# GpSimd's order of row gathers and indirect adds, written by an estimate of its time

## The chip, the cores and the metric

One core of one Trainium2 chip runs the kernel. The metric is device microseconds of one execution, the median of several runs. The engines are TensorE (PE, with its weight loads as PEld), VectorE (DVE), ScalarE (ACT), GpSimd (POOL) and the sequencer SyncE (SP), which issues most loads. Sixteen DMA engines move the data of all queues.

## The reference, cut to what matters

The layer has a token mixer (attention and a recurrent branch) and then PEER, a channel mixer that retrieves single-neuron experts. All of the change lies in PEER. For 256 tokens:

```python
q = (xt @ w_q).reshape(T, 8, 2, 128)                 # 8 heads, two halves
s = einsum('thcd,hcnd->thcn', q, sub_keys)           # 128 keys for each half
sv, si = top_k(s, 16)
cand = sv[:, :, 0, :, None] + sv[:, :, 1, None, :]   # 16 x 16 candidates
cv, ci = top_k(cand.reshape(T, 8, 256), 16)
idx = i1 * 128 + i2                                  # 16 of 16384 experts for each head and token
g = softmax(cv)
u = u_tab[idx]
act = gelu(einsum('td,ted->te', xt, u)) * g
out = einsum('te,ted->td', act, v_tab[idx])          # then residual add and a last RMSNorm
```

## The kernel before, in words

The token mixer fills the first 638 us. PEER follows in two phases.

**The u phase** is a list of 144 **units**, run in order u = 0 to 143. A unit streams one 1 MB tile of weights through TensorE. A query unit (`wq`, 16 of them, two for a head) makes a head's queries for all 256 tokens. A `u` unit (128 of them) multiplies 128 experts' rows of `u_tab` with the first TD = 192 tokens and stores the gelu of it. So for 192 tokens every expert is computed densely; the weights g are scattered into a dense matrix `G` in HBM (three tensors `g_d`, one for each 64 tokens), and later multiply the dense gelu.

**The v phase** (128 chunks of 1 MB, u = 144 to 271) multiplies the weighted gelu with `v_tab` densely.

The last 64 tokens go another way: their experts' rows are **gathered**. Each head has 8 gathers of 128 rows (1 MB each) from `u_tab`, 64 in all, and later as many from `v_tab`. VectorE takes a dot product of each gathered tile with the tokens (`dot`, L605), and in the v phase a scaled add (`axpy`, L623).

Work in one unit, in the order in which it is written (this order is the order on every engine; the section is scheduled by hand, `tc.manual_schedule()`):

1. TensorE: the unit's matmuls (L125). Then ACT copies a part of PSUM (`rest`, L798) and VectorE adds (`total`, L803). The `rest` copy marks a unit's end in the trace.
2. ACT rounds the tile of unit u+3 (`whi`, L566).
3. `want_rows(u)` (L594): GpSimd issues row gathers, while there are requests and one of the 4 `rows` buffers is counted as free (its dot was written two units earlier, or more).
4. `add_some`: GpSimd issues indirect adds to `g_d` (L635). A head has 24: 8 for each of the three tensors. The first add of a head to a tensor waits until all adds of the head before to that tensor have landed (`wait_for`).
5. `bg.run(budget)`: VectorE's retrieval steps (`retrieve`, the top-16 work of a head), while their written costs stay within a budget.
6. `use_rows(u, budget)`: the dots, each against a credit of 2.4, and only for rows requested at least LAG units earlier.
7. VectorE subtracts to get the low part of the tile of unit u+3 (`wlo`, L570). TensorE's unit u+3 needs it. SP then issues the load of unit u+7.

When a head's retrieval has finished, `spread` (called through `later`) sends its indices and weights to the tile `two`, from which both gathers and adds read, and appends 8 gathers to `wanted` and 24 adds to `to_add`.

`scores` (L679), the matmuls of a head's queries with its keys, stand behind a unit's matmuls, two units after the head's second query unit (`due`). At u = 135 and 137 SP loads the first tiles of `G` (`load_G`); the first of these loads waits for all adds of the last head. `weigh` and `weighed` at u = 140 and 141 prepare the first operand `a` of the v phase.

Of the kernel before, what the change touches and what calls it, by code (L numbers as in the profile page):

```python
# [22 lines left out]
HEADS = 8  # L23
# [8 lines left out]
KEEP = 6  # L32
BUDGET = 2.9
BUDGET_Q = 2.7
BUDGET_U = 1.05
ROWS_WQ = 0.5
ROWS_U = 1.0
ROWS_U2 = 1.35
ROWS_V = 1.25
ROWS = 4  # L40
RAW = 4
LAG = 4
PRIO = 300

# [34 lines left out]
def body(tc, A, out):  # L79
# [3 lines left out]
    with ExitStack() as es:  # L83
# [33 lines left out]
        def w_stationary(p, w, x, ks=range(KT), n=T):  # L117
            hi, lo = (t.rearrange("p (k c) -> p k c", c=128) for t in w)
            for k in ks:
                ins = [(p[:, 0:2 * n].rearrange("p (a t) -> p a t", t=n), hi[:, k], x[:, k, :, 0:n]),  # L120
                       (p[:, 0:n], lo[:, k], x[:, k, 0, 0:n])]
                if k == ks[-1]:
                    ins.reverse()
                for i, (d, a, m) in enumerate(ins):
                    pe.matmul(d, a, m, start=k == ks[0] and i == 0, stop=k == ks[-1] and i == 1)  # L125
# [10 lines left out]
        def bank(tag):  # L136
            return ps.tile([128, 512], F32, name=tag)
# [408 lines left out]

        units = [("wq", i) for i in range(6)]
        for h in range(3, HEADS):
            units += [("u", 10 * (h - 3) + i) for i in range(10)] + [("wq", 2 * h), ("wq", 2 * h + 1)]
        units += [("u", i) for i in range(10 * (HEADS - 3), 128)]  # L550
        stream = [A[name][i] for name, i in units]
        order = list(range(32 - KEEP, 32)) + list(range(32 - KEEP))
        stream += [A["v"][g, q] for g in order for q in range(4)]
# [2 lines left out]
        def fetch(i):  # L556
            if i < len(stream):
                raws[i] = (wp.tile([128, 2048], F32, name="raw") if i % RAW < 3 else
                           gp.tile([128, 2048], F32, name="raw4"))
                nc.sync.dma_start(out=raws[i], in_=stream[i].rearrange("p a b -> p (a b)"))  # L560

        def cut_hi(i, c=slice(0, 2048)):
            if i < len(stream):
                if i not in his:
                    his[i], los[i] = (wp.tile([128, 2048], F32R, name=n) for n in ("whi", "wlo"))
                act.activation(his[i][:, c], raws[i][:, c], AF.Copy)  # L566
# [5 lines left out]

        wanted, coming, later = [], [], []
        free, used = [0] * ROWS, []
        credit = 0.0

        def use_rows(u, budget):
            nonlocal credit
            for f in later:
                f()  # L580
            later.clear()
            credit = min(credit + budget, 3.0)
            while credit > 0 and coming and coming[0][0] <= u - LAG:
                _, t, f = coming.pop(0)
                f(t)
                used.append(u)
                credit -= 2.4

        def want_rows(u):
            while wanted and (free or used and used[0] <= u - 2):  # L590
                free.pop() if free else used.pop(0)
                table, idx, f = wanted.pop(0)
                t = gp.tile([128, D], F32, name="rows", bufs=ROWS)
                nc.gpsimd.indirect_dma_start(out=t, out_offset=None, in_=table,  # L594
                                             in_offset=bass.IndirectOffsetOnAxis(ap=idx, axis=0))
                coming.append((u, t, f))
# [34 lines left out]
        to_add = []  # L631
        added = {}

        def add_one(h, tt, at, gw):
            ins = nc.gpsimd.indirect_dma_start(  # L635
                out=cells[tt], out_offset=bass.IndirectOffsetOnAxis(ap=at, axis=0),
                in_=gw, in_offset=None, compute_op=ALU.add).ins
            mine = added.setdefault((h, tt), [])
            tc.add_to_no_dep_group(f"adds{h}{tt}", ins)
            if mine:  # L640
                tc.declare_no_dep(ins, group=f"adds{h}{tt}", reason="different experts of one head")
            elif h:
                wait_for(ins, h - 1, tt)
            mine.append(ins)

        def wait_for(ins, h, tt):
            for i in added[h, tt]:
                tc.add_manual_dep(ins, i.name, mybir.DependencyInfo(
                    mybir.DependencyClass.Sync, mybir.DependencyReason.DATA), reason="adds to G")

        def add_some(n):
            for _ in range(n):
                if to_add:
                    add_one(*to_add.pop(0))


        def spread(h, made):
# [17 lines left out]
        def scores(h, qT, keys):  # L675
            sp = bank("sx")
            for i in range(4):
                tt, c = i // 2, i % 2
                pe.matmul(sp[:, i * 128:(i + 1) * 128], qT[c][:, tt * 128:(tt + 1) * 128],  # L679
                          keys[:, c], start=True, stop=True)  # L680
            s = rp.tile([128, 4, 128], F32, name="s", bufs=2)
            act.activation(s.rearrange("p a n -> p (a n)"), sp, AF.Copy)
            bg.queue.append(retrieve(h, s))
# [53 lines left out]

        for i in range(3 + RAW):
            fetch(i)
# [12 lines left out]
        qT, due = [], []  # L752
        prods, Gs = {}, {}

        def load_G(m):
            Gs[m] = G = [vp.tile([128, 4, 64], F32, name=f"G{b}") for b in range(TD // 64)]
            g = order[m]
            for b in range(TD // 64):
                ins = nc.sync.dma_start(out=G[b], in_=g_d[b][:, 4 * g:4 * g + 4, :]).ins
                if m == 0:  # L760
                    wait_for(ins, HEADS - 1, b)

        def weigh(n):
            x, G = stash.pop(order[n]), Gs.pop(n)
            prods[n] = x
            for b in range(TD // 64):
                c = slice(64 * b, 64 * b + 64)
                dve.tensor_tensor(x[:, :, c], x[:, :, c], G[b], op=ALU.mult)
# [14 lines left out]
                stash[n] = x  # L783

        vp = None
        for u, (name, i) in enumerate(units):
            query = name == "wq"
            n = T if query else TD
            g, j = i // 4, i % 4
            if query and i % 2 == 0:  # L790
                keys = rp.tile([128, 2, 128], F32, name="keys")
                nc.scalar.dma_start(out=keys, in_=A["keys"][:, i:i + 2])
            p = bank("mm")
            w_stationary(p, (his.pop(u), los.pop(u)), hT, n=n)
            while due and due[0][0] <= u - 2:
                due.pop(0)[1]()
            rest = sm.tile([128, T], F32, name="rest")[:, 0:n]
            act.activation(rest, p[:, n:2 * n], AF.Copy)  # L798
            if query:
                y = rp.tile([128, T], F32, name=f"qT{i % 2}", bufs=1)  # L800
            else:
                y = sm.tile([128, T], F32, name="total")[:, 0:n]
            dve.tensor_tensor(y, p[:, 0:n], rest, op=ALU.add)  # L803
            cut_hi(u + 3)
            if query:
                qT.append(y)
                if i % 2:
                    due.append((u, lambda h=i // 2, q=qT, k=keys: scores(h, q, k)))
                    qT = []
            else:  # L810
                if j == 0:
                    st = stp.tile([128, 4, TD], F32, name="stash")
                act.activation(st[:, j], y, AF.Gelu_apprx_tanh)
                if j == 3:
                    if g < 32 - KEEP:
                        nc.scalar.dma_start(out=spill_d[g], in_=st)
                    else:
                        stash[g] = st
            busy = len(sel) < HEADS
            want_rows(u)  # L820
            add_some(2 if u % 4 else 1)
            bg.run(BUDGET_Q if query else BUDGET_U)
            use_rows(u, ROWS_WQ if query else ROWS_U if busy else ROWS_U2)
            if not busy and not to_add and vp is None:
                rp_cm.__exit__(None, None, None)
                kp_cm.__exit__(None, None, None)
                vp = es.enter_context(tc.tile_pool(name="v", bufs=2))
            if u == 135:
                load_G(0)
            if u == 137:  # L830
                load_G(1)
            if u == 140:
                weigh(0)
            if u == 141:
                a = weighed(0)
                refill(0)
            cut_lo(u + 3)
            fetch(u + 3 + RAW)
        assert not to_add and not bg.queue
# [20 lines left out]
        for n in range(31):  # L860
            for q in range(4):
                u = 144 + 4 * n + q
# [13 lines left out]
                cut_lo(u + 3)  # L876
                fetch(u + 3 + RAW)
            a = a1
# [146 lines left out]
```

## Time and profile before

| | us |
|---|---|
| median of 3 runs | 1984.75 |
| lowest and highest run | 1983.99, 1991.14 |
| the profiled execution | 1982.2 |
| span in its trace, first to last instruction | 1980.4 |

| engine | busy us | share of the span |
|---|---|---|
| PE | 1908.7 | 96% |
| DVE | 1550.9 | 78% |
| ACT | 972.4 | 49% |
| POOL | 705.9 | 36% |

Busy time is the union of an engine's instructions. A busy PE need not be at full speed, since its clock has two levels, and matmuls' ends are modelled. The shares are means over the whole kernel; which engine is late in a stage has to be read from that stage.

### The profile page before, as it was taken

What the parts mean: (1) busy time and instruction counts of PE and PEld (TensorE: products, weight loads), DVE (VectorE), ACT (ScalarE), POOL (GpSimd) and SP (SyncE); (2) the same over time, 40 slices, a digit from 0 to 9 for tenths busy, and PEclk for the clock granted to TensorE, in tenths of its full rate; (3) what the DMA queues carried; (4) which work ended last, traced back from release to release, by engine and by line L of the source; (5) the groups of instructions that cost most, each with busy time, mean ns of one, the idle gap of its engine ahead of it and who ended that gap; (6) DMA issues with size and microseconds to landing.
All of it is one profiled execution on the core that took longest, in us unless ns stands there. A gap on an engine that the chain in (4) does not pass through costs nothing. (4 is left out here: it accounts for less than half of the span.)

```text
span 1980.4 us, 26958 instructions
## 1 busy us (share of the span) xinstructions
PE 1908.7 (96%) x10570; PEld 1698.4 (86%) x10570; DVE 1550.9 (78%) x1884; ACT 972.4 (49%) x1115; POOL 705.9 (36%) x347
## 2 busy tenths in 40 slices
PE   7999999999999999999999889999999999999996
PEld 6888888888887899999999888899888888888884
DVE  7876655566556799999998666788888888888885
ACT  5554554444434555555565344455444444444443
POOL 1000000000000077888887888832332333233320
PEclk9999999999999999999999899999999999999998
DMA  7579555555555689999999989999999999999992
GB/s 294 194 264 331 189 207 191 180 185 190 193 211 184 227 306 344 302 302 302 331 317 318 290 306 318 342 406 389 369 410 402 379 392 407 408 384 390 379 395 86
DMA packets 142638, 594.71 MB, mean 300 GB/s; under 512 B 48768, under 2 KB 62128, under 8 KB 76464
## 3 DMA queue, kind: packets, MB, share of 16 engines
q1 hardware_dynamic: 82624, 422.72, 58.2%
q0 software_dynamic: 47936, 145.36, 20.8%
q10 hardware_dynamic: 11952, 24.92, 3.3%
q8 instruction: 83, 1.36, 0.3%
q14 instruction: 43, 0.35, 0.0%
HBM read 564.51 MB, written 28.68 MB: 300 GB/s over the span
## 5 line engine op out<-in xcount | busy, mean ns | idle before, releaser
L125 PE MATMUL mm<-hT,whi 128*128 128x384 f32 (+1 forms) x3328 | 1051.7, 378 | 0.2 <-ACT whi L93 0.2
L125 PE MATMUL mm<-hT,wlo 128*128 128x192 f32 (+1 forms) x3328 | 851.8, 266 | 35.9 <-DVE wlo L570 35.4
L125 PEld LDWEIGHTS mm<-hT,wlo 128*128 128x128 f32 x3328 | 638.9, 192 | 49.0 <-DVE wlo L570 41.0
L566 ACT ACTIVATE whi<-raw 128x2048 fp32r<-128x2048 f32 (+1 forms) x281 | 521.5, 1859 | 315.5 <-PE pv L857 205.4
L125 PEld LDWEIGHTS mm<-hT,whi 128*128 128x128 f32 x3328 | 622.0, 191 | 52.5 <-ACT hT L214 0.6
L570 DVE TENSOR_TENSOR wlo<-raw,whi 128x2048 fp32r<-128x2048 f32 (+1 forms) x281 | 620.9, 2217 | 37.9 <-ACT whi L566 37.9
L635 POOL DMA_INDIRECT g_d<-two x192 | 407.6, 2123 | 74.3 <-issue 70.0
L94 DVE TENSOR_TENSOR wlo<-raw,whi 128x2048 fp32r<-128x2048 f32 (+1 forms) x122 | 239.5, 1973 | 113.3 <-ACT whi L93 113.1
L594 POOL DMA_INDIRECT rows<-v_rows,two x64 | 173.8, 2716 | 382.9 <-DVE accv L623 349.2
L93 ACT ACTIVATE whi<-raw 128x2048 fp32r<-128x2048 f32 (+1 forms) x122 | 200.6, 1657 | 56.5 <-PE mm L114 49.8
L853 PE MATMUL pv<-whi,a 128*128 128x512 f32 x512 | 199.7, 390 | 1.0 <-DVE total L803 1.0
L857 PE MATMUL pv<-whi,a 128*128 128x512 f32 x512 | 200.3, 391 | 0.0
L858 PE MATMUL pv<-wlo,a 128*128 128x512 f32 x512 | 199.2, 389 | 0.0
L855 PE MATMUL pv<-wlo,a 128*128 128x512 f32 x512 | 199.2, 389 | 0.0
L854 PE MATMUL pv<-whi,a 128*128 128x512 f32 x512 | 199.2, 389 | 0.0
L605 DVE CUSTOM_DVE_ANT_0 rows<-rows,xg 128x2048 f32<-128x2048 f32 x64 | 146.2, 2285 | 58.8 <-DMA rows<-u_rows,two 58.8
L594 POOL DMA_INDIRECT rows<-u_rows,two x64 | 112.4, 1756 | 134.7 <-ACT rest L798 70.1
L623 DVE SCALAR_TENSOR_TENSOR accv<-rows,hid,accv 128x2048 f32<-128x2048 f32 x63 | 147.9, 2347 | 0.0
L132 ACT ACTIVATE rest<-mm 128x256 f32<-128x256 f32 x96 | 37.0, 385 | 212.4 <-PE mm L125 212.2
L798 ACT ACTIVATE rest<-mm 128x192 f32<-128x192 f32 (+1 forms) x144 | 48.1, 334 | 182.6 <-PE mm L125 180.7
L853 PEld LDWEIGHTS pv<-whi,a 128*128 128x128 f32 x512 | 96.1, 188 | 21.4 <-DVE total L803 1.3
L857 PEld LDWEIGHTS pv<-whi,a 128*128 128x128 f32 x512 | 96.3, 188 | 20.7 <-issue 0.8
(212 smaller groups left out, 1692.5 us busy)
## 6 DMA issues: line engine op xcount, KB each, us to landing
raw<-u SPq DMA_DIRECT2D x128, 1024.0 KB, 6.9
raw<-v SPq DMA_DIRECT2D x128, 1024.0 KB, 8.6
raw<-w_in SPq DMA_DIRECT2D x64, 1024.0 KB, 5.6
raw<-w_branch SPq DMA_DIRECT2D x16, 1024.0 KB, 5.6
raw<-w_out SPq DMA_DIRECT2D x16, 1024.0 KB, 4.9
raw<-wq SPq DMA_DIRECT2D x16, 1024.0 KB, 7.8
g_d<-zeros ACTq DMA_DIRECT2D x12, 1024.0 KB
G<-g_d SPq DMA_DIRECT2D x96, 128.0 KB, 9.9
```

Of the source, the lines that this page charges most:

```text
L93: return (act.activation(dst_hi, src, AF.Copy), dve.tensor_tensor(dst_lo, src, dst_hi.bitcast(F32), op=ALU.subtract))
L94: dve.tensor_tensor(dst_lo, src, dst_hi.bitcast(F32), op=ALU.subtract))
L125: pe.matmul(d, a, m, start=k == ks[0] and i == 0, stop=k == ks[-1] and i == 1)
L566: act.activation(his[i][:, c], raws[i][:, c], AF.Copy)
L570: dve.tensor_tensor(los[i][:, c], raws[i][:, c], his[i][:, c].bitcast(F32), op=ALU.subtract)
L594: nc.gpsimd.indirect_dma_start(out=t, out_offset=None, in_=table, in_offset=bass.IndirectOffsetOnAxis(ap=idx, axis=0))
L635: ins = nc.gpsimd.indirect_dma_start(out=cells[tt], out_offset=bass.IndirectOffsetOnAxis(ap=at, axis=0), in_=gw, in_offset=None, compute_o ...
L853: pe.matmul(p, a[:, j, 0:128], hi[:, j], start=first, stop=False)
L854: pe.matmul(p, a[:, j, 256:384], hi[:, j], start=False, stop=False)
L855: pe.matmul(p, a[:, j, 0:128], lo[:, j], start=False, stop=last)
L857: pe.matmul(p, a[:, j, 128:256], hi[:, j], start=first, stop=False)
L858: pe.matmul(p, a[:, j, 128:256], lo[:, j], start=False, stop=last)
```

## The change

The new code is in the section on PEER alone. It does these things:

- GpSimd's adds are no longer two in a unit (one in every fourth). A number `pool_at` estimates how far GpSimd has been given work, 2.1 us for a gather and 2.4 us for an add; `now` estimates when a unit ends, 5.6 us for a query unit and 4.6 us for a `u` unit. A unit first issues its gathers and then adds as long as `pool_at` lies before the unit's estimated end. From u = 137 on all remaining adds would be issued.
- There are 12 `u` units between two heads' query units, in place of 10.
- The budgets of retrieval and dots in a unit change a little.
- Rows are used at least five units after their request (LAG + 1) up to u = 143, in place of four.
- The scores of the first head stand one unit earlier.
- `load_G`, `weigh` and `weighed` stand one to three units later.

```diff
-BUDGET_U = 1.05
+BUDGET_U = 0.9
-ROWS_U = 1.0
-ROWS_U2 = 1.35
+ROWS_U = 1.08
+ROWS_U2 = 1.25
+UNIT_Q = 5.6
+UNIT_U = 4.6
+ADD_US = 2.4
+ROW_US = 2.1
...
-            units += [("u", 10 * (h - 3) + i) for i in range(10)] + [("wq", 2 * h), ("wq", 2 * h + 1)]
-        units += [("u", i) for i in range(10 * (HEADS - 3), 128)]
+            units += [("u", 12 * (h - 3) + i) for i in range(12)] + [("wq", 2 * h), ("wq", 2 * h + 1)]
+        units += [("u", i) for i in range(12 * (HEADS - 3), 128)]
...
-            while credit > 0 and coming and coming[0][0] <= u - LAG:
+            while credit > 0 and coming and coming[0][0] <= u - (LAG + 1 if u < 144 else LAG):
...
                 table, idx, f = wanted.pop(0)
+                pool_at += ROW_US
...
-        def add_some(n):
-            for _ in range(n):
-                if to_add:
-                    add_one(*to_add.pop(0))
+        def add_some(end):
+            nonlocal pool_at
+            while to_add and pool_at < end:
+                pool_at += ADD_US
+                add_one(*to_add.pop(0))
...
-            while due and due[0][0] <= u - 2:
+            while due and due[0][0] <= u - (2 if u > 2 else 1):
...
+            pool_at = max(pool_at, now)
+            now += UNIT_Q if query else UNIT_U
             want_rows(u)
-            add_some(2 if u % 4 else 1)
+            add_some(now if u < 137 else 1e9)
...
-            if u == 135:
+            if u == 138:
                 load_G(0)
-            if u == 137:
+            if u == 139:
                 load_G(1)
-            if u == 140:
+            if u == 141:
                 weigh(0)
-            if u == 141:
+            if u == 142:
```

GpSimd, from the first add of the last head on (the number behind `two` names a head's tile; the three `g_d` are the tensors of 64 tokens each). Before, from unit 106, with gathers of head 5 (counted from 0) between the adds:

```order
L635 DMA g_d_213<-two_10196 1048576x1
L635 DMA g_d_214<-two_10196 1048576x1
L635 DMA g_d_215<-two_10196 1048576x1
L635 DMA g_d_213<-two_10196 1048576x1
L594 DMA rows<-u_rows,two_8944 128x2048
L635 DMA g_d_214<-two_10196 1048576x1
L635 DMA g_d_215<-two_10196 1048576x1
L635 DMA g_d_213<-two_10196 1048576x1
L594 DMA rows<-u_rows,two_8944 128x2048
```

Now, from unit 116, the same adds, with gathers of head 6 between them:

```order
L642 DMA g_d_213<-two_10480 1048576x1
L642 DMA g_d_214<-two_10480 1048576x1
L601 DMA rows<-u_rows,two_9691 128x2048
L642 DMA g_d_215<-two_10480 1048576x1
L642 DMA g_d_213<-two_10480 1048576x1
L642 DMA g_d_214<-two_10480 1048576x1
L601 DMA rows<-u_rows,two_9691 128x2048
L642 DMA g_d_215<-two_10480 1048576x1
L642 DMA g_d_213<-two_10480 1048576x1
```

Three adds stand between two gathers in place of three or four, and at a given add of the last head the gathers are a head further on.

VectorE, the start of the u phase. Before, the query sums (`qT`) of units 0 to 3, and then the first retrieval steps:

```order
L803 TENSOR_TENSOR qT_5475<-mm,rest 128x256
L570 TENSOR_TENSOR wlo<-raw_5374,whi 128x2048
L803 TENSOR_TENSOR qT_5518<-mm,rest 128x256
L570 TENSOR_TENSOR wlo<-raw,whi 128x2048
L803 TENSOR_TENSOR qT_5563<-mm,rest 128x256
L570 TENSOR_TENSOR wlo<-raw,whi 128x2048
L803 TENSOR_TENSOR qT_5613<-mm,rest 128x256
L668 MAX sv<-s 128x8
```

Now:

```order
L813 TENSOR_TENSOR qT_5475<-mm,rest 128x256
L574 TENSOR_TENSOR wlo<-raw_5374,whi 128x2048
L813 TENSOR_TENSOR qT_5518<-mm,rest 128x256
L574 TENSOR_TENSOR wlo<-raw,whi 128x2048
L813 TENSOR_TENSOR qT_5570<-mm,rest 128x256
L677 MAX sv<-s 128x8
```

The retrieval of the first head starts in unit 2 in place of unit 3.

Written out unit by unit by the rules above, the two programs stand like this (numbers issued up to and with that unit):

| up to unit | dots before, now | gathers before, now | adds before, now |
|---|---|---|---|
| 87 | 30, 33 | 33, 36 | 137, 127 |
| 92 | 33, 35 | 36, 38 | 145, 134 |
| 121 | 49, 50 | 52, 53 | 192, 177 |
| 131 | 55, 55 | 58, 58 | 192, 192 |
| 143 | 62, 61 | 65, 64 | 192, 192 |

The first four gathers stand in unit 8 (before: 10), the last add in unit 131 (before: 119), and the last head's retrieval ends in unit 92 (before: 86). From unit 92 on a dot stands in about every second unit; of these 27 dots 8 stand five units behind their gather, 15 six and 4 seven. Before, of the 20 dots in units 90 to 124, 16 stand five units behind, 3 six and 1 seven.

## Rows read from the trace of the kernel before

**Rows 1.** All `rest` copies (L798): durations ns min/median/max, first and last start in us.
```profile
L798 ACT ACTIVATE rest<-mm x144: 308/332/387, 638.6 to 1370.6; 128x192 f32<-128x192 f32 x128, 128x256 f32<-128x256 f32 x16
```

**Rows 2.** Three stretches: us, busy (x instructions) by engine, PEclk, DMA share, GB/s.
```profile
691.90:1074.80 382.90, 376.24 (x2538) 365.69 (x2537) 369.67 (x649) 216.41 (x288) 311.77 (x154) 1.00 0.95 316
1074.80:1272.60 197.80, 171.36 (x1123) 169.13 (x1122) 132.20 (x114) 85.31 (x109) 170.08 (x87) 0.94 0.92 310
1272.60:1370.60 98.00, 97.86 (x671) 97.60 (x669) 83.39 (x73) 51.25 (x67) 39.29 (x18) 0.97 1.00 390
```

**Rows 3.** The first stretch, `rest` copies alone: ACT busy us and count.
```profile
691.90:1074.80 382.90, 26.06 (x78) 1.00 0.95 316
```

**Rows 4.** Waits in 1074.8 to 1272.6: us in total, times, longest.
```profile
PE mm L125 <- DVE wlo L570: 26.4, 7, 5.7
DVE rows L605 <- DMA rows<-u_rows,two: 58.5, 11, 9.7
```

**Rows 5.** Timeline of `rest` copies, units 7, 9, 28, 29, 130, 131: start, us, [idle before].
```profile
684.70 0.32 ACT L798 ACTIVATE rest<-mm 128x192 f32<-128x192 f32 x1
...
691.87 0.33 ACT L798 ACTIVATE rest<-mm 128x192 f32<-128x192 f32 x1 [2.05 <-PE mm L125]
...
787.57 0.39 ACT L798 ACTIVATE rest<-mm 128x256 f32<-128x256 f32 x1 [3.21 <-PE mm L125]
...
793.21 0.38 ACT L798 ACTIVATE rest<-mm 128x256 f32<-128x256 f32 x1 [1.32 <-PE mm L125]
...
1311.37 0.33 ACT L798 ACTIVATE rest<-mm 128x192 f32<-128x192 f32 x1 [2.17 <-PE mm L125]
...
1315.92 0.33 ACT L798 ACTIVATE rest<-mm 128x192 f32<-128x192 f32 x1 [2.17 <-PE mm L125]
```

**Rows 6.** Timeline of VectorE, units 129 and 130.
```profile
1307.18 0.36 DVE L803 TENSOR_TENSOR total<-mm,rest 128x192 f32<-128x192 f32 x1 [0.45 <-ACT rest L798]
1307.45 2.28 DVE L605 CUSTOM_DVE_ANT_0 rows<-rows,xg 128x2048 f32<-128x2048 f32 x1
...
1309.66 2.29 DVE L570 TENSOR_TENSOR wlo<-raw,whi 128x2048 fp32r<-128x2048 f32 x1
1311.86 0.35 DVE L803 TENSOR_TENSOR total<-mm,rest 128x192 f32<-128x192 f32 x1
1313.53 2.29 DVE L570 TENSOR_TENSOR wlo<-raw,whi 128x2048 fp32r<-128x2048 f32 x1 [1.32 <-ACT whi L566]
```

**Rows 7.** Unit 115's `rest`, its gather on GpSimd, the dot of that gather.
```profile
1235.09 0.33 ACT L798 ACTIVATE rest<-mm 128x192 f32<-128x192 f32 x1
...
1256.13 1.37 POOL L594 DMA_INDIRECT rows<-u_rows,two  x1 [0.31 <-issue]
...
1267.52 2.29 DVE L605 CUSTOM_DVE_ANT_0 rows<-rows,xg 128x2048 f32<-128x2048 f32 x1 [8.08 <-DMA rows<-u_rows,two]
```

**Rows 8.** GpSimd's timeline: first gather, first add, longest head wait, last add.
```profile
702.09 1.03 POOL L594 DMA_INDIRECT rows<-u_rows,two  x1 [70.13 <-ACT rest L798]
...
711.14 1.62 POOL L635 DMA_INDIRECT g_d<-two  x1 [0.30 <-issue]
...
1070.45 3.60 POOL L635 DMA_INDIRECT g_d<-two  x1 [6.32 <-issue]
...
1278.68 1.91 POOL L635 DMA_INDIRECT g_d<-two  x1 [0.30 <-issue]
```

**Rows 9.** The page's groups of adds and gathers: busy us, mean ns | idle before.
```profile
L635 POOL DMA_INDIRECT g_d<-two x192 | 407.6, 2123 | 74.3 <-issue 70.0
...
L594 POOL DMA_INDIRECT rows<-u_rows,two x64 | 112.4, 1756 | 134.7 <-ACT rest L798 70.1
```

**Rows 10.** An add on GpSimd while VectorE stands still, and VectorE's next instruction.
```profile
1108.38 1.54 POOL L635 DMA_INDIRECT g_d<-two  x1 [0.30 <-issue]
...
1113.95 2.29 DVE L605 CUSTOM_DVE_ANT_0 rows<-rows,xg 128x2048 f32<-128x2048 f32 x1 [9.71 <-DMA rows<-u_rows,two]
```

**Rows 11.** Windows of 50 us, adds alone (POOL busy, count): the slowest window.
```profile
1250.00:1300.00 50.00, 23.19 (x10) 0.93 0.94 348
```

More of the change, by code (lines that the diff above doesn't have):

```diff
@@ L574, in body @@
         free, used = [0] * ROWS, []
+        pool_at = 0.0
         credit = 0.0
@@ L649, in wait_for @@
                     mybir.DependencyClass.Sync, mybir.DependencyReason.DATA), reason="adds to G")
-        def add_some(n):
-            for _ in range(n):
-                if to_add:
-                    add_one(*to_add.pop(0))
+        def add_some(end):
+            nonlocal pool_at
+            while to_add and pool_at < end:
+                pool_at += ADD_US
+                add_one(*to_add.pop(0))
         def spread(h, made):
@@ L785, in body @@
         vp = None
+        now = 0.0
         for u, (name, i) in enumerate(units):
```

## The prediction

> **What bounds the kernel now.** I read the u phase by stages first, since its 144 `rest` copies give a clock of units: unit 0 ends at 638.6 us and unit 143 at 1370.6 [rows 1]. That is 732 us for 143 units. A `u` unit that nothing holds up takes 1315.92 - 1311.37 = 4.55 us, a query unit 793.21 - 787.57 = 5.64 [rows 5]. With 15 query units and 128 `u` units the phase could take 85 + 582 = 667 us, so about 65 us are lost in it.
>
> Where they go, by the windows [rows 2]:
>
> - 691.9 to 1074.8 holds the 78 units 10 to 87 [rows 3], 10 of them query units: 68 x 4.55 + 10 x 5.64 = 366 us, measured 382.9. VectorE is busy for 369.67 of these, so the 17 us lost are VectorE's: retrieval, dots and `wlo` together are more than a unit's time.
> - 1074.8 to 1272.6 holds the 35 units 88 to 122, at best 159 us, measured 197.8. Here VectorE is busy only 67%. It stands for 58.5 us before dots whose rows have not landed, in 11 waits; behind the dot stands `wlo`, and TensorE waits 26.4 us for that [rows 4]. TensorE's granted clock is a mean of 0.94 there, that is, stretches at the lower of its two levels behind these waits [rows 2]; 6% of 198 us is the other 12. Together 38 us: the largest loss, and the place at which the change is aimed.
> - 1272.6 to 1370.6 is clean: the units run at 4.55 us, with the DMA engines at a share of 1.00 and 390 GB/s [rows 2].
>
> Why the rows are late is seen in GpSimd. The gather that belongs to unit 115 (`rest` at 1235.09) starts at 1256.13, 21.0 us late, and its dot starts 11.4 us after that, having waited 8.08 [rows 7]. GpSimd works without a break from 702.09 to 1280.6 [rows 8]: an add takes 2.12 us and 0.30 of pause, a gather from `u_rows` 1.76 and 0.30 [rows 9]. Before, two units hold on average 3.5 adds and a gather, 3.5 x 2.42 + 2.06 = 10.5 us, while two `u` units take 9.1. So the program gives GpSimd more than it can do, its lag grows from head to head, and from unit 88 on it is longer than the units between gather and dot.
>
> **The change, part by part.**
>
> *GpSimd's order.* Two units now get about 3 adds and a gather: 9.3 us, still 2% over 9.1, but in units where VectorE holds the pace to 4.8 us it is below. The ledger: the first gather now stands two units earlier. Before, it started 702.09 - 691.87 = 10.2 us after unit 9 [rows 5, 8], the unit in which the first head was spread; now that unit is 7 (684.70), so GpSimd starts at 694.9. The first add follows 711.14 - 702.09 = 9.05 us later, 704.0. From first to last add took 1280.6 - 711.1 = 569.5 us before, with 47 gathers between and the head waits in it (the longest 6.32 [rows 8]); now 54 gathers lie between, 7 x 2.06 = 14.4 more. The last add then ends at 704.0 + 583.9 = 1288. No add or gather is saved.
>
> *VectorE, units 8 to 92.* This stretch now holds what 10 to 87 held (the retrieval of heads 1 to 7, of which the ends lie alike): 85 units in place of 78, all seven more being `u` units, and 35 dots in place of 30. On VectorE a `wlo` takes 1311.86 - 1309.66 = 2.20 us, a `total` 0.27 and a dot 2.21 from start to start [rows 6]. So 382.9 + 7 x 2.47 + 5 x 2.21 = 411.3 us, if VectorE stays the bound. TensorE would want 75 x 4.55 + 10 x 5.64 = 397.7; this is the lower bound for the stretch, if smaller budgets for each unit take all waiting away. I take 411.3, since the work is the same and its spread over units differs by a few per cent. Unit 92 ends at 684.7 + 411.3 = 1096.0.
>
> *Units 93 to 143.* All 51 are `u` units: at 4.55 us, 232.1. VectorE needs two `wlo`, two `total` and a dot in two units, 7.15 of 9.1 us [rows 6], so it holds nothing up. Unit 143 would end at 1328.1, in place of 1370.6: 42.5 us gained before any late row.
>
> *Late rows that remain.* Unit 131, the last with adds, ends at 1096.0 + 39 x 4.55 = 1273.5, and its last add on GpSimd at 1288: a lag of 14.5 us. How much lag a dot bears: it stands 0.49 + 0.27 us behind its unit's `rest` [rows 5, 6], so six units behind its gather leave 27.3 + 0.8 = 28.1 us; less the 11.4 from gather to dot [rows 7], 16.7. Five units leave 12.1. So most rows come just in time, and a head wait of up to 6 us near the end makes a few late. The price lies between 0 and 6 to 7 us: the upper end if the last 58 adds are slower (next paragraph). I take 5.
>
> *A rule against the change.* While VectorE stands still, an add takes 1.54 us [rows 10]; on the mean 2.12 [rows 9]. So part of GpSimd's pace before was lent by the very waits that the change removes. With VectorE busy for 7.15 of 9.1 us I put the late adds between 2.12 and the slowest window's 23.19 / 10 = 2.32 [rows 11], nearer 2.25 at worst; 58 x 0.13 = 7.5 us more lag, 22 in all, which is 5.3 over 16.7. [...]
>
> *Small parts.* Scores one unit earlier: the first retrieval starts one unit earlier, in a stretch with VectorE idle; worth 0 to 4 us, counted as 0. `load_G` at 138: the last add ends at 1288, unit 138 at 1305; SP isn't held up. `weigh` and `weighed` one unit later leave a unit (4.55 us) for the operand `a`; 0 to 2 us. The v phase has the same loads, rows and dots but for one dot more.
>
> **Sum.** 42.5 - 5 = 37.5 us. The profiled execution takes 1982.2 us, 1.8 more than its span, and lies 2.5 below the median of the runs: 1982.2 - 37.5 = 1944.7 in its terms, 1984.75 - 37.5 = 1947 as a median.
>
> **The rivals.**
>
> 1. *GpSimd stays the bound.* If every add takes 2.25 us with its waits, the last one ends 192 x 0.13 = 25 us later, at 1313. Late rows then tie the units to it: unit 131 ends 16.7 before, and 12 units of 4.55 follow: 1313 - 16.7 + 54.6 = 1351, a gain of 20, median 1965. For it: adds are quick when VectorE stands. Against: between 691.9 and 1074.8 VectorE was 97% busy, and GpSimd's lag grew there mostly by the surplus of adds [rows 2].
> 2. *The DMA engines.* With adds and rows they moved 316 GB/s at a share of 0.95 [rows 2]. If 333 is all they can do with adds among the packets, a unit with 1.05 MB of weights, half a gather and 0.1 MB of spilled gelu (1.67 MB) takes 5.0 us instead of 4.55, over the 39 units 93 to 131: 18 us. Rows then come in time, since GpSimd gains on the units: 42.5 - 18 = 24.5, median 1960. Against it: 390 GB/s right after the adds end [rows 2].
> 3. *Not faster, or slower.* The same tie to GpSimd as in 1, with dearer adds. Unit 143 ends at 1370.6 again when the last add ends at 1332.7, 44.7 us later: 0.233 us an add, 2.36 in all. At 2.41 the kernel is 0.5% slower (1995). For it: one window of 50 us at 2.32 [rows 11]. Against: that window holds 10 adds; it would have to be the mean of all 192.
> 4. *More than forecast.* VectorE's overload in 8 to 92 goes too: 13.6 us more, and no late row: 1984.75 - 56 = 1929. Against: retrieval and dots are as many as before, and VectorE was 97% busy.
>
> **Chances.** The forecast (1938 to 1957) has 0.62; rival 1 (1957 to 1975) 0.15; rival 2 (1955 to 1970) 0.08; rival 3 0.09, of which 0.04 is slower by over 0.5%; rival 4 (below 1938) 0.06. The runs of before differ by 0.36%, so about 0.5%, 10 us, can be told from no change. Under 1975 lies all but rival 3 and a tail of rival 1: faster 0.88, within 0.5% 0.08, slower 0.04. The range reaches down to 1933, where two thirds of VectorE's overload are gone and no row is late, and up to 1970, where adds cost 2.28 us; some 0.14 are left out above and 0.04 below.
>
> **What the profile after would show.** Units 8 to 92 take some 411 us with VectorE over 95% busy (398 would be rival 4). VectorE's waits for rows fall from 58.5 us to under 15, and TensorE's for `wlo` behind them from 26.4 to under 8, with a granted clock near 1.00 from unit 93 to 131. GpSimd's last add ends near 1288 and stands about 15 us after its unit. If adds after unit 92 take over 2.25 us, and lag passes 17, it is rival 1 or 3; if units there take 5 us, with loads late and VectorE not waiting for rows, rival 2. The prediction is wrong if the lag comes from something other than the number of adds, such as longer head waits or rows that take 15 us to land when the units run at full pace.

## The result, and the profile after

The changed kernel takes 1954.68 us (median of 4 runs, 1951.76 to 1962.11) beside 1987.45 us of the kernel before in the same runs: a ratio of 0.984 (95% interval 0.9805 to 0.9876). Run once more, it took 1957.52 us (1956.16 to 1960.8) beside 1983.84: 0.9864 (0.985 to 0.9878). So it is 26 to 33 us faster; 37.5 were forecast. The profiled execution took 1953.84 us, with a span of 1952.1.

The `rest` copies of units 7, 92, 131 and 143 in the timeline of the changed kernel, which answer to [rows 1, 5] (`rest` is now L808, `total` L813, `wlo` L574, `whi` L570, the dot L612, the gather L601, the add L642):

```profile
680.83 0.32 ACT L808 ACTIVATE rest<-mm 128x192 f32<-128x192 f32 x1
...
1092.65 0.33 ACT L808 ACTIVATE rest<-mm 128x192 f32<-128x192 f32 x1 [1.52 <-PE mm L129]
...
1276.41 0.33 ACT L808 ACTIVATE rest<-mm 128x192 f32<-128x192 f32 x1 [2.16 <-PE mm L129]
...
1334.38 0.31 ACT L808 ACTIVATE rest<-mm 128x192 f32<-128x192 f32 x1
```

Its windows over units 9 to 92, units 93 to 143, 20 us from the hand-over to v, and 20 us in the tail (columns as in [rows 2]):

```profile
684.60:1092.60 408.00, 403.30 (x2729) 392.23 (x2728) 396.13 (x666) 231.10 (x307) 338.58 (x168) 1.00 0.97 331
1092.60:1334.40 241.80, 233.75 (x1633) 232.23 (x1631) 190.09 (x166) 124.61 (x158) 197.21 (x90) 1.00 0.99 354
...
1334.50:1354.50 20.00, 16.45 (x62) 13.39 (x63) 13.40 (x14) 7.38 (x7) 0.93 (x1) 0.79 1.01 404
...
1906.50:1926.50 20.00, 13.46 (x40) 8.59 (x39) 13.91 (x14) 5.51 (x10) 0.00 (x0) 0.74 0.12 47
```

Its waits from 1092.6 to 1334.4, which answer to [rows 4], and from 1325 to 1420, the start of v (us in total, times, longest):

```profile
DVE rows L612 <- DMA rows<-u_rows,two: 26.0, 10, 6.0
PE mm L129 <- DVE wlo L574: 4.6, 3, 2.5
...
PE pv L865 <- DVE total L813: 7.1, 1, 7.1
ACT whi L570 <- DMA raw<-v: 5.5, 2, 4.7
```

GpSimd's timeline there: first gather, first add, last add, and the first gather after it [rows 8]:

```profile
692.64 1.03 POOL L601 DMA_INDIRECT rows<-u_rows,two  x1 [60.43 <-ACT stash L823]
...
700.31 1.62 POOL L642 DMA_INDIRECT g_d<-two  x1 [0.30 <-issue]
...
1300.82 1.54 POOL L642 DMA_INDIRECT g_d<-two  x1 [0.30 <-issue]
1302.67 1.00 POOL L601 DMA_INDIRECT rows<-u_rows,two  x1 [0.30 <-issue]
```

Windows of the adds alone in the changed kernel (POOL busy, count, then clock, DMA share, GB/s):

```profile
684.60:1092.60 408.00, 283.60 (x131) 1.00 0.97 331
1092.60:1304.00 211.40, 147.70 (x62) 1.00 0.98 349
```

How to read them. The unit clock gives where the 28.3 us between the two spans (1980.4 and 1952.1) came from. Up to unit 143, 1370.56 - 1334.38 = 36.2 us are gained; after it, 7.9 are lost again, since v takes 617.7 us from there to the end in place of 609.8. The waits show the gain's place: VectorE's for rows fell from 58.5 to 26.0 us, and TensorE's for `wlo` behind them from 26.4 to 4.6, with the granted clock at 1.00 where it was 0.94. VectorE is still busy 97% of units 9 to 92 (396.13 of 408). The adds after unit 92 are the surprise: 147.70 / 62 = 2.38 us each, where before they took 2.12 there.

| stretch | forecast us | measured us |
|---|---|---|
| unit 7 ends at | 684.7 | 680.8 |
| units 8 to 92 | 411.3 | 411.8 |
| units 93 to 143 | 237.1 | 241.7 |
| gain up to unit 143 | 37.5 | 36.2 |
| lost in v | 0 | 7.9 |

### The profile page after: what moved, and what is told of

The parts are those of the page before. It is cut to its first block, busy times and chain, and to the rows that moved or that the text cites. A ratio compares the mean times of both kernels' runs of the same rounds, so it can differ in the third digit from the quotient of the medians.

```text
span 1952.1 us, 26942 instructions
## 1 busy us (share of the span) xinstructions
PE 1898.3 (97%) x10570; PEld 1687.3 (86%) x10570; DVE 1550.7 (79%) x1884; ACT 973.1 (50%) x1115; POOL 731.2 (37%) x347
## 5 line engine op out<-in xcount | busy, mean ns | idle before, releaser
L129 PE MATMUL mm<-hT,whi 128*128 128x384 f32 (+1 forms) x3328 | 1038.2, 375 | 0.2 <-ACT whi L97 0.2
L570 ACT ACTIVATE whi<-raw 128x2048 fp32r<-128x2048 f32 (+1 forms) x281 | 521.6, 1860 | 322.1 <-PE pv L869 235.8
L129 PEld LDWEIGHTS mm<-hT,whi 128*128 128x128 f32 x3328 | 614.3, 188 | 52.5 <-ACT hT L218 0.6
L129 PEld LDWEIGHTS mm<-hT,wlo 128*128 128x128 f32 x3328 | 631.3, 190 | 23.2 <-DVE wlo L574 15.4
L574 DVE TENSOR_TENSOR wlo<-raw,whi 128x2048 fp32r<-128x2048 f32 (+1 forms) x281 | 620.1, 2215 | 33.2 <-ACT whi L570 33.1
L642 POOL DMA_INDIRECT g_d<-two x192 | 431.3, 2246 | 70.6 <-issue 58.0
L601 POOL DMA_INDIRECT rows<-v_rows,two x64 | 184.2, 2879 | 383.5 <-DVE accv L630 341.3
L612 DVE CUSTOM_DVE_ANT_0 rows<-rows,xg 128x2048 f32<-128x2048 f32 x64 | 146.1, 2284 | 26.3 <-DMA rows<-u_rows,two 26.0
L601 POOL DMA_INDIRECT rows<-u_rows,two x64 | 103.6, 1618 | 85.7 <-ACT stash L823 60.4
L808 ACT ACTIVATE rest<-mm 128x192 f32<-128x192 f32 (+1 forms) x144 | 48.0, 333 | 161.5 <-PE mm L129 157.9
```

The lines of the kernel that those rows point to most:

```text
L574: dve.tensor_tensor(los[i][:, c], raws[i][:, c], his[i][:, c].bitcast(F32), op=ALU.subtract)
L642: ins = nc.gpsimd.indirect_dma_start(out=cells[tt], out_offset=bass.IndirectOffsetOnAxis(ap=at, axis=0), in_=gw, in_offset=None, compute_o ...
```

## The experiments

**The order of the adds alone.** The kernel before with `pool_at` and `now` and the later places of G's loads and the weighing (138, 139, 141 and 142), and nothing of the spread, the fifth unit or the earlier scores:

```diff
...
-            add_some(2 if u % 4 else 1)
+            add_some(now if u < 137 else 1e9)
...
-            if u == 135:
+            if u == 138:
                 load_G(0)
...
```

> The kernel before with GpSimd's new order of adds alone (rows first, adds by the estimate, the G loads and the weighing at 138, 139, 141 and 142); budgets, ten units between queries and the age of the rows stay. My theory: two thirds of the adds in a fixed 2-2-2-1 beat kept GpSimd behind the units, late rows held VectorE and then TensorE, so the new order alone gives most of the gain: 1962 to 1970 us, VectorE's waits for rows after unit 92 fall from 58.5 to under 35 us. Rival: the gain is VectorE's (budgets, twelve units between queries), and the order of the adds alone leaves 1980 us or more.

Measured: 1961.73 us, ratio 0.9879 (0.9863 to 0.9895), 23.7 us faster. Its waits in units 93 to 143:

```profile
DVE rows L612 <- DMA rows<-u_rows,two: 27.3, 9, 8.1
...
PE mm L129 <- DVE wlo L574: 7.9, 3, 4.3
```

**The even spread alone.** The kernel before with the budgets and twelve units:

```diff
-BUDGET_U = 1.05
-ROWS_U = 1.0
-ROWS_U2 = 1.35
+BUDGET_U = 0.9
+ROWS_U = 1.08
+ROWS_U2 = 1.25
...
-            units += [("u", 10 * (h - 3) + i) for i in range(10)] + [("wq", 2 * h), ("wq", 2 * h + 1)]
+            units += [("u", 12 * (h - 3) + i) for i in range(12)] + [("wq", 2 * h), ("wq", 2 * h + 1)]
```

> The kernel before with the even spread alone (twelve u units between queries, budgets 0.9, 1.08 and 1.25), adds still 2-2-2-1 a unit. My theory: GpSimd still has more to do in a unit than a unit lasts, so rows stay late and the time stays near that of before, 1985 us within 8. Rival: the spread is what gave the gain, 1955 to 1960 us.

Measured: 1990.12 us, ratio 1.0027 (1.001 to 1.0044). The waits of before stand as they were:

```profile
DVE rows L605 <- DMA rows<-u_rows,two: 50.5, 11, 9.4
PE mm L125 <- DVE wlo L570: 25.7, 7, 6.9
```

These two decide between the theories: the order of the adds gives 24 of the 26 to 33 us by itself, the spread gives nothing by itself. What the other parts add on top of the order (0.9879 beside 0.984 and 0.9864) is small, and the intervals overlap. Most of it can be the earlier scores: unit 7 ends at 685.1 us with the order alone and at 680.8 in the changed kernel, while units 8 to 92 take 411.0 and 411.8.

**Rows used four units on again.**

```diff
-            while credit > 0 and coming and coming[0][0] <= u - (LAG + 1 if u < 144 else LAG):
+            while credit > 0 and coming and coming[0][0] <= u - LAG:
```

> The changed kernel with rows used four units on again. My theory: the ring of four row buffers and the dots' own cadence already set the distance from gather to dot (in the program 5 to 7 units in either), so nothing changes: the changed kernel's time within 2 us. Rival: the fifth unit is what removes the waits for rows, and without it the time is 5 to 10 us above the changed kernel's.

Measured: 1952.19 us, ratio 0.983 (0.981 to 0.985): the fifth unit gives nothing. Its trace showed something else. In the tail, TensorE waits for the last scaled adds before the matmul that takes `accv`. In the changed kernel that row of TensorE's timeline is

```profile
1913.89 2.05 PE L915 MATMUL pv<-accv,rows 128*128 128x512 f32 x2 [6.54 <-issue]
```

and with rows used four units on

```profile
1918.41 2.05 PE L915 MATMUL pv<-accv,rows 128*128 128x512 f32 x2 [5.01 <-issue]
```

and in the kernel before

```profile
1943.47 2.04 PE L903 MATMUL pv<-accv,rows 128*128 128x512 f32 x2 [5.01 <-issue]
```

In all 14 traces of this study that wait has three lengths: 5.01 us in the kernel before and four others with four units, 6.54 in all eight with five, and 8.92 in the spread alone. In the program these kernels have 62, 61 and 60 dots up to unit 143: what isn't done there is done in v and shifts its scaled adds. With the lower clock behind the longer wait (0.74 in the window of the tail above, 0.91 in the 20 us from 1936.3 in the kernel before), the last 96 matmuls and the end take 49.4 us in the changed kernel, 46.7 before and 46.6 here. Over all traces with four units and the new order it is 46.6 to 47.3, over those with five 48.0 to 49.5.

**Half of the adds.**

```diff
-                          for k in range(8) for b in range(TD // 64))
+                          for k in range(4) for b in range(TD // 64))
```

> The changed kernel with half of each head's adds into G left out (so its output is not the reference's). My theory: late adds of 2.38 us put GpSimd 22 to 25 us behind from unit 109 on; with half of them it stays in step, VectorE's waits for rows after unit 92 (26.0 us) and the 7.1 us wait of TensorE at the hand-over to v go, units 8 to 92 stay at 408 to 412 us since VectorE sets them, and the time is 1938 to 1942 us. Rival: GpSimd is no longer what holds units 93 to 143 and the hand-over's loss is the G loads' own, so the time stays near 1952 us.

Measured: 1944.48 us, ratio 0.979 (0.9775 to 0.9805), 10 to 13 us below the changed kernel and 2.5 above what I expected. VectorE's wait for rows after unit 92 is gone and no unit there takes over 5 us. So the adds still hold units 93 to 143 in the changed kernel; the rival falls. Half of the adds is also half of their packets in the DMA engines, and this run doesn't tell the two apart; the order alone, which gains 24 us with every add in place, does so for the larger part. TensorE's wait at the hand-over fell from 7.1 to 2.2 us and didn't go.

**`a` ahead of the cut.**

```diff
+            if u == 142:
+                a = weighed(0)
+                refill(0)
             cut_hi(u + 3)
...
-            if u == 142:
-                a = weighed(0)
-                refill(0)
             cut_lo(u + 3)
```

> The changed kernel with the weighed first stage of v (a) written ahead of unit 142's cut on ScalarE. My theory: at the hand-over a stood on ScalarE behind whi, which waited 4.74 us for v's raw rows, and TensorE waited 7.1 us for what comes of a; put ahead, the wait falls to about 3 us and 3 to 5 us come back: about 1949 us. Rival: a waits for G by itself (until 1325.7 us and after), so the order on ScalarE gives nothing or only moves the wait to whi: within 1.5 us of the changed kernel.

Measured: 1953.36 us, 0.9842 (0.9823 to 0.986). TensorE's wait fell to 4.1 us (to about 3 was expected), but the 3 to 5 us can't be seen in the time: with `a` already done, the last unit's `rest` and `total` on ScalarE and VectorE still stand behind the same `whi`, which waits 2.8 us for v's tile. The rival holds.

**Row buffers free one unit earlier.**

```diff
-            while wanted and (free or used and used[0] <= u - 2):
+            while wanted and (free or used and used[0] <= u - (1 if u < 144 else 2)):
```

> The changed kernel with a row buffer counted free one unit after its dot in place of two, so that gathers are issued a unit earlier (in the program 6 to 8 units ahead of their dot in place of 5 to 7). My theory: rows are late by GpSimd's lag of 22 to 25 us, so a unit more (4.6 us) takes most of VectorE's 26.0 us of waits for rows after unit 92 away, to 5 to 8 us, and 4 to 6 us of time: about 1948 us. Rival: the gather then waits on GpSimd for the dot that frees its buffer, and GpSimd loses as much as VectorE gains: within 2 us of the changed kernel, or above it.

Measured: 1946.31 us, 0.9801 (0.9784 to 0.9817), as the first theory has it. But its trace (of the slowest of its seven runs, 1954.78) shows 26.1 us of waits for rows in place of 26.0, so the mechanism isn't seen; and the three further kernels with this edit, below, gave 0.9824, 0.9859 and 0.9871. I leave it open.

**A higher estimate for late adds** (2.6 us from unit 92 on):

```diff
+ADD_LATE = 2.6
...
-                pool_at += ADD_US
+                pool_at += ADD_US if CUR[0] < 92 else ADD_LATE
...
+            CUR[0] = u
...
```

> The changed kernel with the planner's estimate of an add raised from 2.4 to 2.6 from unit 92 on, so that adds are spread to unit 135. My theory: the lag stays near 15 us in place of 24, the waits for rows go, about 5 us come back before unit 140, but the last adds land near the G loads and a part may be lost there: 1946 to 1953 us. Rival: the adds end later and hold the G loads, TensorE's wait at the hand-over grows by what is saved: 1953 us or more.

Measured: 1949.32 us, 0.9823 (0.9805 to 0.9841): inside what was expected, and not apart from the changed kernel. In its trace VectorE still waits 20.2 us for rows, and 7.4 more before one dot.

**Both, `a` first and buffers free earlier.**

```diff
-            while wanted and (free or used and used[0] <= u - 2):
+            while wanted and (free or used and used[0] <= u - (1 if u < 144 else 2)):
...
+            if u == 142:
+                a = weighed(0)
+                refill(0)
             cut_hi(u + 3)
...
-            if u == 142:
-                a = weighed(0)
-                refill(0)
             cut_lo(u + 3)
```

> The changed kernel with a ahead of the cut in unit 142 and row buffers free a unit earlier. My theory: the two losses lie in different stretches (units 93 to 143 and the hand-over) and add up: about 1944 us. Rival: rows in time make GpSimd end no sooner, the hand-over stays what it was, and the sum is that of the better one alone: 1948 us or more.

Measured: 1952.95 us, 0.9824 (0.9801 to 0.9848). They don't add up: that is above the 1946.31 us of the earlier buffers alone.

**The changed kernel again,** with no edit.

> The changed kernel itself, once more, on the chip of the next three. My theory: rows later than their dot come and go from run to run (242 to 245 us in units 93 to 143 among kernels of one order of adds), so its median is 1951 to 1956 us. Rival: the runs so far were on a slower chip, and it stands at 1946 to 1949 us, like the kernels with small edits.

Measured: 1957.52 us (above), just over the first theory's range and far from the rival's. Its trace is worth more than its time. The window of units 93 to 143, and the waits in it:

```profile
1092.60:1345.50 252.90, 241.01 (x1632) 238.85 (x1631) 191.36 (x169) 123.94 (x157) 197.13 (x94) 0.97 0.96 343
```

```profile
DVE rows L612 <- DMA rows<-u_rows,two: 35.3, 8, 7.3
...
PE mm L129 <- DVE wlo L574: 11.8, 6, 3.9
```

The same program took 11 us more in the same 51 units than in its first trace, and 4.2 less in v. It stood at the same place at unit 92 (1092.63), but GpSimd's lag there, the start of unit 94's gather less that unit's `rest`, was 19.8 us in place of 10.7.

**Earlier buffers and four units.**

```diff
-            while credit > 0 and coming and coming[0][0] <= u - (LAG + 1 if u < 144 else LAG):
+            while credit > 0 and coming and coming[0][0] <= u - LAG:
...
-            while wanted and (free or used and used[0] <= u - 2):
+            while wanted and (free or used and used[0] <= u - (1 if u < 144 else 2)):
```

> The changed kernel with row buffers free one unit after their dot and rows used four units on. My theory: the fifth unit gives the u phase nothing, but it leaves one dot more for the v phase, shifts the scaled adds there, and the last two of them then hold TensorE 8 us in place of 5.4 before the last matmuls; without it the tail falls from 34.5 to 31.7 us, so 2.5 to 3 us come back on top of what the earlier gathers give: 1944 to 1950 us, and a tail of 31.7 us in the trace. Rival: the tail's length depends on how the u phase ended, not on the number of dots: a tail of 34 us and the time within 2 us of the kernel with earlier gathers alone (1946.3).

Measured: 1956.78 us (1943.99 to 1961.31), 0.9859 (0.9833 to 0.9884). The tail, by the last 96 matmuls and the end, is 46.6 us with the wait of 5.01, 2.8 below the changed kernel as the first theory says; the time isn't what either expected.

**G's first loads earlier,** on top of the two edits above.

```diff
-            if u == 138:
+            if u == 136:
                 load_G(0)
-            if u == 139:
+            if u == 138:
                 load_G(1)
-            if u == 141:
+            if u == 140:
                 weigh(0)
-            if u == 142:
+            if u == 141:
                 a = weighed(0)
```

> The kernel with buffers free a unit earlier and rows used four units on, and G's first loads in units 136 and 138, the weighing at 140 and 141 (two, one, one and one units earlier). My theory: G's first loads stand too late for the hand-over to v, where loads already fill the DMA engines, and a comes late by that; earlier, TensorE's wait there falls under 2 us and the first 20 matmuls of v from 8 to 10 us after unit 143 to about 6: 2 to 3 us faster than with the later places. Rival: the first load of G waits on SP for the last adds, at unit 137, so the next tile's load is late in its place, and the time is the same or up to 5 us above.

Measured: 1957.91 us, 0.9871 (0.9855 to 0.9887). SP waits 10.8 us for the adds to G, and TensorE 7.8 at the hand-over: the rival's mechanism, at no price that can be told.

**Half of the adds, with G's loads where they were before.** On top of the edit with half the adds:

```diff
-            if u == 138:
+            if u == 135:
                 load_G(0)
-            if u == 139:
+            if u == 137:
                 load_G(1)
-            if u == 141:
+            if u == 140:
                 weigh(0)
-            if u == 142:
+            if u == 141:
                 a = weighed(0)
```

> The changed kernel with half of each head's adds left out (its output isn't the reference's) and G's loads and the weighing back at the units of before (135, 137, 140, 141). With half the adds GpSimd has no backlog and nothing waits for adds there, so the place alone is tested. My theory: the place is what still costs at the hand-over with half the adds (first 20 matmuls of v 7.9 us after unit 143, 5.3 in the kernel before); with the old place they are back near 5.3 and the time is 2 to 3 us below the other kernel with half the adds (1944.5). Rival: the loss comes from units that run at full pace up to the hand-over with all loads behind the DMA engines, whatever the place: 7 to 8 us, and no gain.

Measured: 1941.4 us, 0.9796 (0.9779 to 0.9814), the ratio of the other kernel with half the adds, 0.979. The 20th matmul of v starts 8.3 us after the `rest` of unit 143 (10.4 in the changed kernel, 8.0 in the other kernel with half the adds), not 5.3 or 5.4 as before: the place of G's loads is not it. Units 93 to 143 run at full pace:

```profile
1092.80:1325.10 232.30, 231.82 (x1630) 231.56 (x1628) 191.11 (x168) 123.78 (x158) 96.75 (x39) 1.00 0.97 371
```

What is left at the hand-over stands in its VectorE timeline, ahead of the first matmul of v at 1327.00:

```profile
1322.18 2.28 DVE L612 CUSTOM_DVE_ANT_0 rows<-rows,xg 128x2048 f32<-128x2048 f32 x1
...
1324.39 2.29 DVE L574 TENSOR_TENSOR wlo<-raw,whi 128x2048 fp32r<-128x2048 f32 x1
1326.59 0.35 DVE L813 TENSOR_TENSOR total<-mm,rest 128x192 f32<-128x192 f32 x1
```

```profile
1327.00 0.50 PE L865 MATMUL pv<-whi,a 128*128 128x512 f32 x1 [2.37 <-DVE total L813]
```

TensorE's first matmul of v waits for the `total` of unit 143, and that stands behind a dot in unit 142. In the kernel before, the dots fell in units 141 and 143, and the wait was 1.03 us:

```profile
1371.50 0.50 PE L853 MATMUL pv<-whi,a 128*128 128x512 f32 x1 [1.03 <-DVE total L803]
```

With the dot in 142 and no gathers behind time, it is 2.2 to 2.4 us, in both kernels with half the adds and in the spread alone. No run moves that dot by itself.

## Why the prediction was right, and where its steps were not

**What bounds, and GpSimd's order: right, and shown.** Late rows behind too many adds were the loss, and the order alone takes most of it away; the spread alone takes none. Rival 4 (VectorE's overload gone) and rival 2 (the DMA engines) didn't come: units 8 to 92 took 411.8 us, as VectorE's ledger says, and with half the adds the units after 92 ran at full pace with the DMA engines moving 371 GB/s.

**The first head's scores, counted as 0,** were worth 3.9 us: unit 7 ended at 680.8 (forecast 684.7). It ended at 685.1 and 685.2 in the order alone and the spread alone, which lack this part. Of the 36.2 us gained up to unit 143, these 3.9 stood in no term of the sum.

**Late rows that remain: the mechanism was right, the add's price was mis-sized, and the bill came out near by luck.** I put the late adds at 2.12 us, at worst 2.25; they took 2.38. So the last add ended at 1302.4 us, not 1288, which is 26.0 behind unit 131 (1276.41), not 14.5; it started 1300.82 - 1276.41 = 24.4 behind. The text's own sign for rival 1 (over 2.25 us, lag past 17) was there, but not its price. I had let all that a lag exceeds 16.7 us become time, which by 26.0 would be 9.3; in fact VectorE, busy for 79% of that stretch, hid most of the 26.0 us it waited. Units of 4.55 us would take 232.1; of the 9.6 above that, 3.3 are the last unit (7.9 us from `rest` to `rest`, a matter of the hand-over), so late rows cost 6.3 in this trace, where 5 was forecast. The `rest` copies of units 117 to 119, and ScalarE's instruction ahead of the second, show such a delay:

```profile
1206.88 0.33 ACT L808 ACTIVATE rest<-mm 128x192 f32<-128x192 f32 x1 [2.17 <-PE mm L129]
...
1215.01 0.21 ACT L615 ACTIVATE hid<-hid 128x8 f32<-128x8 f32 x1 [5.75 <-DVE hid L612]
1215.12 0.31 ACT L808 ACTIVATE rest<-mm 128x192 f32<-128x192 f32 x1
...
1217.75 0.31 ACT L808 ACTIVATE rest<-mm 128x192 f32<-128x192 f32 x1
```

8.2 us, then 2.6: only ScalarE's copy was late, behind the gelu (`hid`) of a head whose last dot was late; TensorE was busy through all of the 8.2 us, and with the next unit (1221.99) the three lose 1.5 us over 3 x 4.55. Counted for all but the last unit, late rows cost 6 to 21 us in the ten traces with the new order and all adds (20.8 in the second trace of the same program), and 3.9 and 0.2 us of small delays remain with half of the adds. A size that varies so much between runs isn't known to a microsecond, whatever one trace says.

**Why late adds got dearer.** Laid beside VectorE's timeline, the 62 adds after unit 92 fall apart: the 6 that met no VectorE work took 1.55 us on the mean, the 28 that met it for 90% of their time or more 2.52 (1.57 to 3.65), and the 28 between 2.44. Before, of 59 such adds, 15 met none and took 1.55, 25 met it for 90% or more and took 2.52, and the 19 between took 2.04. At both ends the prices are the same, and the shares moved; those between met VectorE for 65% of their time, 54% before, and got dearer. So the waits that the change removed had lent GpSimd its pace, as the prediction's paragraph "A rule against the change" said, only more than the slowest window showed. This goes by what ran at the same time; no run changes VectorE's work alone, and none shows by which path it makes an add dearer.

**The step that failed: v at no cost.** The text said "the same loads, rows and dots but for one dot more" and put nothing beside it. v lost 7.9 us: 2.8 in the tail, which is just that dot, by the wait of 6.54 in place of 5.01 and the lower clock behind it (0.74 and 0.91 in the two windows of the tail above); and 5.1 at its start. Of these, 2.7 lie ahead of the first matmul of v, which started 3.7 us after the `rest` of unit 143 in place of 0.9; and 2.3 lie in its first 20 matmuls, at a granted clock of 0.50 in the first 5 us (1.00 before) and 0.63 us a matmul (0.39 before), after a wait of 7.1 us. There the chain of waits of the changed kernel reads (start, us, what):

```profile
1315.10 16.45 DMA raw<-v
...
1331.58 0.03 ACT whi L570
...
1333.74 0.74 ACT a L783
...
1337.65 0.36 DVE total L813
...
1338.05 0.79 PE pv L865
```

A tile of v took 16.45 us to land; in the kernel before, one there took 9.2, and 8.6 is the median of v on its page. SyncE issued it among G's loads:

```profile
1310.92 1.64 SPq L768 DMA_DIRECT2D G<-g_d  x3
1315.10 0.33 SPq L564 DMA_DIRECT2D raw<-v  x1
1315.77 2.40 SPq L768 DMA_DIRECT2D G<-g_d  x3
```

GpSimd, at last through with its adds, issued five gathers from 1302.67 to 1313.14. `whi`, `a`, `rest` and `total` of the last unit stood in line behind the tile. The ten traces with all adds and the new order fall apart here by GpSimd's backlog, the lag of the last add's start behind its own unit. In the six with a lag of 20 to 26 us, `whi` waited 2.3 to 6.7 us for tiles of v ahead of the hand-over, and TensorE 4.1 to 7.8. In the four with a lag of 13 to 17, the second trace of the changed kernel (15.3) among them, `whi` waited at most 0.8 and TensorE 2.2 to 3.2; with half of the adds it is 0, and 2.2 and 2.4. So the late tile goes with the backlog, and the rest with the dot's place in unit 142. That the gathers held up the tile is argued, not tried by itself. The late tile also made the last unit 3.3 us longer, and without it, with half of the adds, the start of v still lost 2.7 and 3.0 us: so it cost some 5.5 us in this trace, and nothing in the second.

No kernel with all the work is shown to beat the changed one by more than its own runs differ. Half of the adds, at about 1943 us, shows what a GpSimd in time could still give at most: some 10 to 13 us.

## What to carry to other kernels

Here GpSimd, which issues the gathers and adds, went at a pace that followed what VectorE did (1.55 us an add beside an idle VectorE, 2.52 on the mean beside a busy one): when a change takes stalls away from VectorE, price GpSimd's instructions by the rows in which VectorE is busy, not by their mean over the stretch with the stalls. Data that came just in time made a time that varied: the same program's two traces differed by 11 us in one stretch, so a small edit there needs many runs, and a trace of one is not a verdict. Look at the seams: moving one small instruction past the end of a phase was hidden in its own phase and cost 2.8 us in the tail of the next.

## What the runs showed of the hardware

- An indirect add took 1.55 us beside an idle VectorE and 2.52 on the mean beside a busy one. Which VectorE work it is seems to matter: up to unit 92, where retrieval's small instructions help to fill VectorE to 97%, the mean was 283.60 / 131 = 2.16, and the 7 adds there that met neither a dot nor a `wlo` took 1.55. In the kernel before, 11 such adds took 1.63, the longest 2.31.
- In windows of 0.5 us the granted clock of TensorE read 1.00 or 0.50 in the traces of both kernels, and a mean between the two only where it changed. In the kernel before, TensorE waited 3.92 us up to 1092.69; the clock was 1.00 up to 1093.0, 0.98 in the next window, 0.50 from 1093.5 to 1096.5, 0.61 in the next, and 1.00 from 1097.0 to 1117.0.
- The length of a short wait of TensorE didn't settle here how long the matmuls behind it took. After 2.25 us at the hand-over, in the second trace of the changed kernel, the matmuls of v took 0.39 to 0.40 us each from the second on, as far as 1351.46:

```profile
1347.68 0.50 PE L865 MATMUL pv<-whi,a 128*128 128x512 f32 x1 [2.25 <-DVE total L813]
1348.01 0.40 PE L866 MATMUL pv<-whi,a 128*128 128x512 f32 x1
```

After 2.17 us, with half of the adds, they took 0.63 from the second on, and 0.39 to 0.40 only from 1336.32:

```profile
1332.86 0.79 PE L865 MATMUL pv<-whi,a 128*128 128x512 f32 x1 [2.17 <-DVE total L813]
1333.45 0.63 PE L866 MATMUL pv<-whi,a 128*128 128x512 f32 x1
```

In both, TensorE was busy for 7.8 of the 10 us before, and the last matmuls of u took 0.25 and 0.36 us. In the five other traces with waits of 2.4 to 3.2 us there, the second matmul of v took 0.39 to 0.45 us, and the seventh 0.63.
